# Block sums for two more gates and a branch, turns and residual loads on another queue, and half of w_out as a double block

## The chip, the cores and the metric

The kernel runs on one core of a Trainium2 chip. The metric is the device time of one execution in microseconds: the median of several timed runs. Beside them one execution was recorded by the profiler; all rows and durations below come from that one. TensorE multiplies matrices into PSUM, VectorE and ScalarE prepare operands and empty PSUM, GpSimd does a few additions, and SP only issues DMAs.

## What is computed

One layer of a hybrid decoder block, for 256 tokens of width 2048, in float32:

```python
h = rmsnorm(x, ln1_w)
proj = h @ w_in                       # q k v | pool input | z | xBC | dt | 3 gates of 2048
merged = (gates[0] * (att @ w_attn_br)      # branch 1, att is 1024 wide
        + gates[1] * (pool @ w_pool_br)     # branch 2, pool is 1024 wide
        + gates[2] * (ssm @ w_ssm_br))      # branch 3, ssm is 2048 wide
x = x + merged @ w_out                      # 2048 x 2048
h2 = rmsnorm(x, ln2_w)
gu = h2 @ w_gate_up                         # 2048 x 11264
x = x + (silu(gu[..., :5632]) * gu[..., 5632:]) @ w_down
return rmsnorm(x, final_w)
```

`gates` is the sigmoid of the last 6144 columns of `proj`.

## The kernel before

Every float32 operand is split into a rounded part `hi` and the rest `lo` (`split`, L139: a rounding on ScalarE, L142, and a difference on VectorE, L143), and a product is three matmuls, hi x hi, hi x lo and lo x hi (`three`, L220). Contraction runs over parts of 128 rows; 2048 rows are 16 of them. The 256 tokens are two tiles of 128, and columns go in blocks of 512. `tokens_block` (L226) makes one block of 512 columns for both token tiles: four rows of weights (1 MB) by one DMA into one of three buffers `raw`, split in two halves into `whi` and `wlo` (five buffers each), then 24 matmuls; a block of 16 rows has 96.

`two_blocks` (L312) makes two blocks of 512 columns at once, in eight pairs of rows. In six pairs it is the plain product, 24 matmuls. In the pairs 0 and 1 the four quarter products (two token tiles by two column blocks, over two rows) are made with seven products in place of eight, 21 matmuls, from sums of the weights (`block_weights`, L286, with the buffers `sraw`, `vu`, `shi`, `slo`) and sums of the activations (`block_forms`, L254). Its order of pairs is 0, 2, 3, 4, 1, 5, 6, 7, and after pair 1 VectorE combines the four accumulators that only the sums use. Before the change it serves `w_gate_up` and `w_down` alone.

PSUM has eight banks: `acc` (four), `tr` (two), `sm` (two). `k4` is a pool of 21 buffers of 4 KB per partition, which holds `h` (8), the parts of `ssm`, `mp` and `x2p` (8 each), `m4` (4), the gates, and others for a while. The pool `early` holds what the first stages use; it is closed after branch 3, and the pool `late` (`sraw`, `shi`, `slo`, `forms`) takes its place.

A block of tokens by channels that a later product contracts over has to be turned (`turn`, L490): 16 DMAs of 32 KB move it to `mid` (`move`), VectorE transposes 32x32 blocks, and it is split into the parts `hi` and `lo` (`parts`). These steps, and `forms_of`, don't stand where they are called: `later` (L120) queues them with a cost, `pause` queues a cost alone, and `side` (L126), called after each half of a weight load, adds a credit (1.4 for 1024 elements, capped at 4) and takes one step off the queue while the credit is positive. `need` (L205) takes steps until the part that is asked for is there. A program, which knows the dependencies, lays the instructions out on the engines and queues from this order.

The stages from 480 us on: branch 2 (gate and product for each of four blocks, L975), `z` and the scan's output with its turn into `ssm` (L985), branch 3 (L1001: two gates, then products and gates in turn; the sums `m4` are turned into `mp` from block 1 on, by SP), `w_out` with the residual (L1018: x loaded by SP into `x2`; four blocks, each turned into `x2p`), and the feed-forward part (L1055).

## Time and profile before

| | us |
|---|---|
| median of 3 timed runs | 1667.23 |
| lowest and highest of them | 1666.58, 1667.69 |
| the profiled execution | 1661.8 |
| its span, first to last instruction | 1660.0 |
| TensorE busy in it | 1632.7 (98%) |
| VectorE busy | 1247.3 (75%) |
| ScalarE busy | 879.0 (53%) |
| GpSimd busy | 59.3 (4%) |

Spans of matmuls overlap, since they are pipelined: the distance from one start to the next is what a matmul takes, not its shown duration. The last column of a row of the timeline, in brackets, is the idle time of the engine before it and what ended that. The window rows give for each engine the busy time in a stretch and the number of its instructions, then the granted share of TensorE's full clock, the busy share of the DMA engines and the GB/s.

### The profile page before, as it was taken

The numbers are of one execution on the slowest core, as the hardware profiler recorded it, in microseconds if no ns is written. First come the engines' busy times: TensorE is split into PE (matmuls) and PEld (weight loads), VectorE is DVE, ScalarE is ACT, GpSimd is POOL, SyncE is SP. The second block draws the span as 40 slices with busy tenths as digits, with TensorE's granted clock in tenths as the row PEclk, the third lists the DMA queues.
The fourth block names the chain that finished last, engine by engine and source line by source line (L and its number), as shares of the span: only waits on it lengthen the run. The fifth ranks groups of instructions, "written<-read, shape, count | busy, mean of one in ns | idle before, by whom it ended". The sixth has DMA issues, their size and how long they took to land.

```text
span 1660.0 us, 20771 instructions
## 1 busy us (share of the span) xinstructions
PE 1632.7 (98%) x7719; PEld 1355.8 (82%) x7719; DVE 1247.3 (75%) x1620; ACT 879.0 (53%) x1161; POOL 59.3 (4%) x58
## 2 busy tenths in 40 slices
PE   9999999999999999999969999999999999999997
PEld 8888888888888888888858888888888888888887
DVE  5789898955764457654547688988879888888986
ACT  6467678544444457544425555554445555445553
POOL 1000001200210000000000000000000000000000
PEclk9999999999999999999989999999999999999999
DMA  8654565556575656665567666666556666656663
GB/s 257 194 167 138 178 196 185 177 178 197 161 242 188 202 164 220 199 228 188 180 204 234 201 212 198 233 215 208 193 196 214 216 215 216 201 195 201 217 213 102
DMA packets 216901, 328.81 MB, mean 198 GB/s; under 512 B 15484, under 2 KB 89472, under 8 KB 216800
## 3 DMA queue, kind: packets, MB, share of 16 engines
q1 hardware_dynamic: 214496, 321.96, 59.5%
q0 software_dynamic: 1552, 4.66, 1.0%
q8 instruction: 60, 0.98, 0.2%
q10 hardware_dynamic: 752, 0.86, 0.2%
q14 instruction: 41, 0.34, 0.1%
HBM read 313.25 MB, written 2.13 MB: 190 GB/s over the span
## 4 chain that ended last, share of the span: by engine, by line
PE 82%; SPq 5%; DVE 5%; DMA 4%; ACT 2%; issue 2%; DVEq 0%; ACTq 0%
PE acc L222 11%; PE acc L223 11%; PE acc L224 11%; PE acc L376 9%; PE tr L222 6%; PE tr L224 5%; PE tr L223 5%; SPq L490 5%; PE sm L223 5%; PE sm L224 5%; PE sm L222 5%; PE acc L377 5%; DVE wlo L143 2%; DMA raw<-in_w_out_dram 1%; ACT whi L142 1%
## 5 line engine op out<-in xcount | busy, mean ns | idle before, releaser
L143 DVE TENSOR_TENSOR wlo<-raw,whi 128x1024 fp32r<-128x1024 f32 (+2 forms) x520 | 626.4, 1217 | 225.2 <-ACT whi L142 220.1
L142 ACT CAST whi<-raw 128x1024 fp32r<-128x1024 f32 (+2 forms) x520 | 529.7, 1035 | 393.5 <-PE acc L224 221.8
L376 PE MATMUL acc<-h,whi 128*128 128x512 f32 x640 | 228.8, 401 | 0.0
L222 PE MATMUL acc<-whi,h 128*128 128x512 f32 (+1 forms) x544 | 210.8, 389 | 2.1 <-DVE sg L920 0.8
L223 PE MATMUL acc<-wlo,h 128*128 128x512 f32 (+1 forms) x544 | 209.2, 385 | 0.6 <-DVE wlo L143 0.5
L224 PE MATMUL acc<-whi,h 128*128 128x512 f32 (+1 forms) x544 | 208.2, 385 | 0.1
L377 PE MATMUL acc<-h,wlo 128*128 128x256 f32 x640 | 180.7, 282 | 0.0
L376 PEld LDWEIGHTS acc<-h,whi 128*128 128x128 f32 x640 | 120.5, 188 | 30.1 <-issue 1.5
L377 PEld LDWEIGHTS acc<-h,wlo 128*128 128x128 f32 x640 | 121.0, 189 | 1.8 <-issue 1.8
L222 PEld LDWEIGHTS acc<-whi,h 128*128 128x128 f32 x544 | 102.0, 188 | 24.2 <-issue 2.3
L222 PE MATMUL tr<-whi,x2p_hi 128*128 128x512 f32 x308 | 120.8, 392 | 0.0
L224 PE MATMUL tr<-whi,x2p_lo 128*128 128x512 f32 x308 | 120.4, 391 | 0.0
L223 PEld LDWEIGHTS acc<-wlo,h 128*128 128x128 f32 x544 | 102.2, 188 | 22.3 <-DVE wlo L143 2.0
L223 PE MATMUL tr<-wlo,x2p_hi 128*128 128x512 f32 x308 | 120.3, 391 | 0.0
L224 PEld LDWEIGHTS acc<-whi,h 128*128 128x128 f32 x544 | 101.7, 188 | 20.7 <-DVE h L146 0.4
L142 ACT CAST whi<-sraw 128x1024 fp32r<-128x1024 f32 x64 | 67.1, 1049 | 90.7 <-PE sm L224 75.4
L143 DVE TENSOR_TENSOR wlo<-sraw,whi 128x1024 fp32r<-128x1024 f32 x64 | 78.2, 1221 | 33.4 <-ACT whi L142 33.2
L222 PE MATMUL sm<-whi,x2p_hi 128*128 128x512 f32 x264 | 102.8, 390 | 0.0
L223 PE MATMUL sm<-wlo,x2p_hi 128*128 128x512 f32 x264 | 102.8, 390 | 0.0
L224 PE MATMUL sm<-whi,x2p_lo 128*128 128x512 f32 x264 | 102.8, 390 | 0.0
L495 DVE STREAM_TRANSPOSE tt<-mid 128x512 f32<-128x512 f32 x46 | 47.3, 1066 | 54.7 <-DMA mid<-ff 18.1
L224 PEld LDWEIGHTS tr<-whi,x2p_lo 128*128 128x128 f32 x308 | 57.9, 188 | 12.8
(311 smaller groups left out, 2855.7 us busy)
## 6 DMA issues: line engine op xcount, KB each, us to landing
raw<-in_w_in_dram SPq DMA_DIRECT2D x104, 1024.0 KB, 5.3
raw<-in_w_gate_up_dram SPq DMA_DIRECT2D x132, 512.0 KB, 4.8
raw<-in_w_down_dram SPq DMA_DIRECT2D x62, 512.0 KB, 5.0
sraw<-in_w_gate_up_dram SPq DMA_DIRECT2D x44, 512.0 KB, 4.6
raw<-in_w_ssm_br_dram SPq DMA_DIRECT2D x16, 1024.0 KB, 5.8
raw<-in_w_out_dram SPq DMA_DIRECT2D x16, 1024.0 KB, 6.4
sraw<-in_w_down_dram SPq DMA_DIRECT2D x20, 512.0 KB, 5.0
raw<-in_w_attn_br_dram SPq DMA_DIRECT2D x8, 1024.0 KB, 5.0
```

The source lines that it names most:

```text
L142: a = act.copy(hi, src)
L143: b = dve.tensor_tensor(lo, src, hi.bitcast(F32), ALU.subtract)
L222: pe.matmul(o, lhsT=xh, rhs=yh, start=first, stop=False)
L223: pe.matmul(o, lhsT=xh, rhs=yl, start=False, stop=False)
L224: pe.matmul(o, lhsT=xl, rhs=yh, start=False, stop=last)
L376: pe.matmul(accs[c], lhsT=hi[:, j, cols], rhs=a.both(k), start=k == 0, stop=False)
L377: pe.matmul(accs[c][:, :SEQ], lhsT=lo[:, j, cols], rhs=a.hi(k), start=False, stop=k == KD - 1)
L490: sp.dma_start(mid[32 * j:32 * j + 32, i], block[32 * i:32 * i + 32, :, j * P:(j + 1) * P])
L495: dve.transpose(tt.rearrange("p k (t i s) -> p t i k s", t=T, i=4)[:, t], mid[:, :, t].rearrange("p i (c k) -> p i k c", k=4),)
```

## The change

- Two gates of branch 2 (blocks 1 and 2), all four gates of branch 3 and all four of its products are made by `two_blocks` with block sums: five double blocks (`two_gates` three times, `two_branches` twice) in place of ten plain blocks.
- `two_blocks` keeps the sums' accumulators in `tr` and `sm` and the others in `acc` (before: the other way round), and takes no forms when `forms` is None: all eight pairs are then plain. The first two blocks of `w_out` are one such double block.
- The four turns of `m4` and the four loads of x into `x2` are issued on GpSimd's queue in place of SP's. Blocks 0 and 1 of `m4` are turned after the last gates, 2 and 3 after the last product. The turns of `x2` stay on SP; those of blocks 0 and 1 now follow each other after the double block.
- `early` is closed and `late` opened before branch 2's products. `vu` moves to `late` with one buffer in place of two, and `k4` has 22 buffers.

```diff
--- before.py
+++ after.py
@@ -87,7 +87,7 @@
 
 
     def k4(shape, dt=F32, name="k4"):
-        return work.tile([P, *shape], dt, tag="k4", name=name, bufs=21)
+        return work.tile([P, *shape], dt, tag="k4", name=name, bufs=22)
 
     def k2(shape, dt=F32, name="k2", tag="k2", bufs=6):
         return work.tile([P, *shape], dt, tag=tag, name=name, bufs=bufs)
@@ -183,6 +183,9 @@
         def __init__(self, n, name):
             self.t = [k4([2, 2, SEQ], F32R, name) for _ in range(n // 2)]
 
+        def need(self, k):
+            pass
+
         def both(self, k):
             return self.t[k // 2][:, k % 2].rearrange("p a s -> p (a s)")
 
@@ -223,17 +226,14 @@
         pe.matmul(o, lhsT=xh, rhs=yl, start=False, stop=False)
         pe.matmul(o, lhsT=xl, rhs=yh, start=False, stop=last)
 
-    def tokens_block(a, nk, loads_of, cols, loaded=None):
-
-        accs = [acc() for _ in range(T)]
+    def tokens_block(a, nk, loads_of, cols, accs=None):
+
+        accs = accs or [acc() for _ in range(T)]
         step = 8 if cols <= 256 else 4
         for i in range(0, nk, step):
             n = min(step, nk - i)
-            if isinstance(a, Parts):
-                a.need(i)
+            a.need(i)
             pieces = weights(loads_of(i, n), [n, cols])
-            if loaded is not None:
-                loaded(i)
             for s, e, hi, lo in pieces:
                 for t in range(T):
                     tok = slice(t * P, (t + 1) * P)
@@ -275,20 +275,23 @@
             later(lambda p=p: forms_of(p), 3.0)
         return out
 
-    def block_loads(w, k, c1, c2):
+    def block_loads(w, k, cols, moved):
 
         k0 = k // 4 * 4
         return [
-            ((lambda r, j=j: r[:, 2 * j:2 * j + 2, :]), turned(w, k0, 4, c, NB)[0][1][:, k - k0:k - k0 + 2, :])
-            for j, c in enumerate((c1, c2))
+            (
+                (lambda r, j=j: r[:, 2 * j:2 * j + 2, :]),
+                turned(w, k0, 4, c, NB)[0][1][:, k - k0:k - k0 + 2, :] if moved else rows(w, k, 2, c, NB),
+            )
+            for j, c in enumerate(cols)
         ]
 
-    def block_weights(w, k, c1, c2):
+    def block_weights(loads):
 
         raw = late.tile([P, 4, NB], F32, tag="sraw", name="sraw", bufs=1)
-        for to, src in block_loads(w, k, c1, c2):
+        for to, src in loads:
             sp.dma_start(to(raw), src)
-        vu = wpool.tile([P, 2, NB], F32, tag="vu", name="vu", bufs=2)
+        vu = late.tile([P, 2, NB], F32, tag="vu", name="vu", bufs=1)
         out = []
 
         def part(src):
@@ -309,16 +312,20 @@
         out.append((hi, lo))
         return out
 
-    def two_blocks(a, forms, w, k0, c1, c2, nk):
-
-
-
-        q1, q7, q5, q6 = acc(), acc(), acc(), acc()
-        q2, q4, q3, q8 = tr(), tr(), sm(), sm()
-        seven = [0, 1]
-        plain = list(range(2, nk // 2))
-        share = len(plain) // len(seven)
-        order = []
+    def two_blocks(a, forms, w, k0, cols, nk, moved=True):
+
+
+
+        if forms is None:
+            q2, q4, q3, q8 = tr(), tr(), sm(), sm()
+            seven, s1, u2, u3, s5 = [], None, None, None, None
+        else:
+            q1, q7, q5, q6 = tr(), tr(), sm(), sm()
+            q2, q4, q3, q8 = acc(), acc(), acc(), acc()
+            seven = [0, 1]
+        plain = list(range(len(seven), nk // 2))
+        share = len(plain) // max(len(seven), 1)
+        order = [] if seven else plain
         for i, p in enumerate(seven):
             order += [p] + plain[i * share:(i + 1) * share]
         for p in order:
@@ -328,7 +335,7 @@
                 while p not in forms:
                     tasks.popleft()[0]()
                 f = forms[p]
-                b11, b21, v, u, z, w_, b22 = block_weights(w, k0 + ka, c1, c2)
+                b11, b21, v, u, z, w_, b22 = block_weights(block_loads(w, k0 + ka, cols, moved))
                 first, last = p == seven[0], p == seven[-1]
                 tok = [slice(t * P, (t + 1) * P) for t in range(T)]
 
@@ -356,14 +363,14 @@
                     dve.tensor_tensor(s5, q5, u2, ALU.subtract)
                     dve.tensor_tensor(u2, q5, u3, ALU.subtract)
             else:
-                for j, (_, _, hi, lo) in enumerate(weights(block_loads(w, k0 + ka, c1, c2), [4, NB])):
+                for j, (_, _, hi, lo) in enumerate(weights(block_loads(w, k0 + ka, cols, moved), [4, NB])):
                     for t in range(T):
                         q = ((q2, q4), (q3, q8))[j][t]
                         for k in range(2):
                             xh, xl = a.hi(ka + k)[:, t * P:(t + 1) * P], a.lo(ka + k)[:, t * P:(t + 1) * P]
                             three(
                                 q, xh, xl, hi[:, k], lo[:, k],
-                                q is q8 and p == plain[0] and k == 0, p == plain[-1] and k == 1,
+                                (q is q8 or not seven) and p == plain[0] and k == 0, p == plain[-1] and k == 1,
                             )
                     side(0.9 * 1024 * SHARE)
         return ((q2, s1), (q4, u3)), ((q3, s5), (q8, u2))
@@ -477,7 +484,7 @@
                     last = split(p[:, k, :], dst.hi(kt), dst.lo(kt), scale(kt))
         return last
 
-    def turn(block, k0, dst, scale=None, wait=5.0):
+    def turn(block, k0, dst, scale=None, queue=sp):
 
 
 
@@ -487,7 +494,7 @@
         def move():
             for i in range(4):
                 for j in range(4):
-                    sp.dma_start(mid[32 * j:32 * j + 32, i], block[32 * i:32 * i + 32, :, j * P:(j + 1) * P])
+                    queue.dma_start(mid[32 * j:32 * j + 32, i], block[32 * i:32 * i + 32, :, j * P:(j + 1) * P])
 
         def parts():
             tt = k4([4, SEQ], F32, "tt")
@@ -505,7 +512,7 @@
             dst.waiting.discard(k0 // 4)
 
         later(move)
-        pause(wait)
+        pause(5.0 if queue is sp else 12.0)
         later(parts, 3.8)
 
 
@@ -909,16 +916,36 @@
             act.activation(sg[:, t, :], a, AF.Sigmoid, scale=rstd1[:, t:t + 1])
         return sg
 
-    def branch(br, j, a_parts, w, sg, loads=plain_loads):
+    def two_gates(br, j):
+
+        c0 = C_G + br * D + j * NB
+        out = []
+        for sums in two_blocks(h, h_forms, w_in, 0, (c0, c0 + NB), KD, False):
+            sg = k4([T, NB], F32, "sg")
+            for t, (q, more) in enumerate(sums):
+                dve.tensor_tensor(more, q, more, ALU.add)
+                act.activation(sg[:, t, :], more, AF.Sigmoid, scale=rstd1[:, t:t + 1])
+            out.append(sg)
+        return out
+
+    def branch(br, j, a_parts, w, sg, banks=None):
         if br == 0:
             m4.append(k4([T, NB], F32, "m"))
         nk = w.shape[0] // P
-        for t, a in enumerate(tokens_block(a_parts, nk, loads(w, 0, j * NB, NB), NB)):
+        for t, a in enumerate(tokens_block(a_parts, nk, plain_loads(w, 0, j * NB, NB), NB, banks)):
             if br == 0:
                 dve.tensor_tensor(m4[j][:, t, :], a, sg[:, t, :], ALU.mult)
             else:
                 dve.tensor_tensor(sg[:, t, :], a, sg[:, t, :], ALU.mult)
-                (dve if br == 2 else pool).tensor_tensor(m4[j][:, t, :], m4[j][:, t, :], sg[:, t, :], ALU.add)
+                pool.tensor_tensor(m4[j][:, t, :], m4[j][:, t, :], sg[:, t, :], ALU.add)
+
+    def two_branches(j, sgs):
+
+        for n, sums in enumerate(two_blocks(ssm, s_forms, ins["w_ssm_br"][0], 0, (j * NB, (j + 1) * NB), KD)):
+            for t, (q, more) in enumerate(sums):
+                dve.tensor_tensor(more, q, more, ALU.add)
+                dve.tensor_tensor(more, more, sgs[n][:, t, :], ALU.mult)
+                dve.tensor_tensor(m4[j + n][:, t, :], m4[j + n][:, t, :], more, ALU.add)
 
     for j in range(4):
         sg = gate(0, j)
@@ -972,12 +999,16 @@
             later(lambda pair=pair: pool_mix(pair), 2.4)
             pair = []
 
-    sg_pool = [gate(1, 0)]
+    sg = gate(1, 0)
     finish_tasks()
-    for j in range(4):
-        if j:
-            sg_pool.append(gate(1, j))
-        branch(1, j, po, ins["w_pool_br"][0], sg_pool[j])
+    early_pool.close()
+    late = ctx.enter_context(tc.tile_pool(name="late", bufs=1))
+    h_forms = block_forms(h, (0, 1))
+    branch(1, 0, po, ins["w_pool_br"][0], sg)
+    sgs = two_gates(1, 1)
+    branch(1, 1, po, ins["w_pool_br"][0], sgs[0], [tr(), tr()])
+    branch(1, 2, po, ins["w_pool_br"][0], sgs[1], [sm(), sm()])
+    branch(1, 3, po, ins["w_pool_br"][0], gate(1, 3))
 
 
     ssg = tiny([T, GROUPS], "ssg", 1)
@@ -998,38 +1029,44 @@
         later(finish, 1.5)
         turn(ys[g], 4 * g, ssm, lambda k: norms[:, 0, k:k + 1])
 
-    sg_ssm = [gate(2, j) for j in range(2)]
+        if g == 0:
+            s_forms = block_forms(ssm, (0, 1))
+
+    sgs = two_gates(2, 0)
     finish_tasks()
-    for j in range(4):
-        branch(2, j, ssm, ins["w_ssm_br"][0], sg_ssm[j], turned_loads)
-        if j + 2 < 4:
-            sg_ssm.append(gate(2, j + 2))
-        if j == 1:
-            mp = Parts(KD, "mp")
-            for i in range(2):
-                turn(m4[i], 4 * i, mp)
-        elif j > 1:
-            turn(m4[j], 4 * j, mp)
-
-    early_pool.close()
-    late = ctx.enter_context(tc.tile_pool(name="late", bufs=1))
+    two_branches(0, sgs)
+    sgs = two_gates(2, 2)
+    mp = Parts(KD, "mp")
+    for j in range(2):
+        turn(m4[j], 4 * j, mp, queue=pool)
+    two_branches(2, sgs)
+    for j in range(2, 4):
+        turn(m4[j], 4 * j, mp, queue=pool)
 
 
     x2 = []
     for j in range(4):
         xj = k4([T, NB], F32, "x2")
-        sp.dma_start(xj, x_in[:, :, j * NB:(j + 1) * NB])
+        pool.dma_start(xj, x_in[:, :, j * NB:(j + 1) * NB])
         x2.append(xj)
     ss2 = tiny([T, 4], "ss2", 1)
     x2p = Parts(KD, "x2p")
-    for j in range(4):
-        for t, a in enumerate(tokens_block(mp, KD, turned_loads(ins["w_out"][0], 0, j * NB, NB), NB)):
+    forms = []
+
+    def residual(j, accs):
+        for t, a in enumerate(accs):
             dve.tensor_tensor(x2[j][:, t, :], a, x2[j][:, t, :], ALU.add)
             junk = k2([NB], F32, "junk")
             act.activation(junk, x2[j][:, t, :], AF.Square, accum_out=ss2[:, t, j:j + 1])
         turn(x2[j], 4 * j, x2p, lambda k: norms[:, 1, k:k + 1])
         if j == 0:
-            forms = block_forms(x2p, (0, 1))
+            forms.append(block_forms(x2p, (0, 1)))
+
+    w_out = ins["w_out"][0]
+    for n, sums in enumerate(two_blocks(mp, None, w_out, 0, (0, NB), KD)):
+        residual(n, [q for q, _ in sums])
+    for j in range(2, 4):
+        residual(j, tokens_block(mp, KD, turned_loads(w_out, 0, j * NB, NB), NB))
     ssum2 = tiny([T], "ssum2", 1)
     dve.tensor_reduce(ssum2, ss2, AX.X, ALU.add)
     rstd2 = rsqrt(ssum2, D, [T], "rs2")
@@ -1056,7 +1093,7 @@
         f = Parts(4 * len(some), "f")
         for i, b in enumerate(some):
             a_ = k4([T, NB], F32, "ff")
-            gates, ups = two_blocks(x2p, forms, wgu, 0, b * NB, DFF + b * NB, KD)
+            gates, ups = two_blocks(x2p, forms[0], wgu, 0, (b * NB, DFF + b * NB), KD)
             for t, (q, more) in enumerate(gates):
                 dve.tensor_tensor(more, q, more, ALU.add)
                 act.activation(a_[:, t, :], more, AF.Silu, scale=rstd2[:, t:t + 1])
@@ -1083,14 +1120,14 @@
                 )
                 fw.extend(fw4[:, c, :] for c in range(4))
         for j in (0,) if last else (0, 2):
-            sums = two_blocks(f, f_forms, wd, k0, j * NB, (j + 1) * NB, nk)
+            sums = two_blocks(f, f_forms, wd, k0, (j * NB, (j + 1) * NB), nk)
             for n in range(2):
                 for q, more in sums[n]:
                     dve.tensor_tensor(more, q, more, ALU.add)
             for n in range(2):
                 down(j + n, 0, NB, j + n if last else None, [more for _, more in sums[n]])
-    down(2, 0, NB, 2, tokens_block(f, nk, turned_loads(wd, k0, 2 * NB, NB), NB))
-    down(3, 0, 256, 3, tokens_block(f, nk, turned_loads(wd, k0, 3 * NB, 256), 256))
+    down(2, 0, NB, 2, tokens_block(f, nk, turned_loads(wd, k0, 2 * NB, NB), NB, [tr(), tr()]))
+    down(3, 0, 256, 3, tokens_block(f, nk, turned_loads(wd, k0, 3 * NB, 256), 256, [sm(), sm()]))
 
 
     wl = []
```

## Rows read from the trace of the kernel before

**Rows 1.** The page's head: busy time by engine, and TensorE's clock by slice.

```profile
PE 1632.7 (98%) x7719; PEld 1355.8 (82%) x7719; DVE 1247.3 (75%) x1620; ACT 879.0 (53%) x1161; POOL 59.3 (4%) x58
...
PEclk9999999999999999999989999999999999999999
```

**Rows 2.** Waits of TensorE, 450 to 1640 us: total, times, longest.

```profile
PE acc L222 <- ACT whi L142: 11.6, 2, 11.0
PE acc L223 <- DVE wlo L143: 1.6, 3, 0.8
PE acc L222 <- DVE sg L920: 0.8, 2, 0.4
PE acc L222 <- DVE x L1027: 0.5, 1, 0.5
```

**Rows 3.** Windows: branch 3's stage, the start of w_out, one feed-forward block.

```profile
700.00:840.00 140.00, 138.76 (x609) 113.65 (x608) 76.38 (x70) 61.76 (x63) 0.00 (x0) 1.00 0.62 196
840.00:880.00 40.00, 27.55 (x112) 21.40 (x111) 21.90 (x21) 13.52 (x14) 0.00 (x0) 0.87 0.76 255
1076.00:1119.00 43.00, 43.00 (x190) 35.36 (x189) 36.81 (x41) 22.47 (x25) 0.00 (x0) 1.00 0.63 213
```

**Rows 4.** Timeline of TensorE: start, duration, line, tiles; w_out's borders and two half blocks.

```profile
845.16 0.39 PE L224 MATMUL acc<-whi,ssm_lo 128*128 128x512 f32 x1
...
939.26 0.39 PE L222 MATMUL acc<-whi,mp_hi 128*128 128x512 f32 x1
...
939.94 0.39 PE L222 MATMUL acc<-whi,mp_hi 128*128 128x512 f32 x1
...
947.42 0.39 PE L222 MATMUL acc<-whi,x2p_hi 128*128 128x512 f32 x1
...
1076.33 0.39 PE L222 MATMUL acc<-whi,x2p_hi 128*128 128x512 f32 x1
...
1097.57 0.39 PE L222 MATMUL acc<-whi,x2p_hi 128*128 128x512 f32 x1
```

**Rows 5.** Timeline of SP's queue, 820 to 905 us.

```profile
825.89 13.21 SPq L490 DMA_DIRECT2D mid<-m  x16
839.20 1.29 SPq L153 DMA_DIRECT2D raw<-in_w_out_dram  x2
...
852.17 10.30 SPq L490 DMA_DIRECT2D mid<-m  x16
862.56 19.93 SPq L153 DMA_DIRECT2D raw<-in_w_out_dram  x7
```

**Rows 6.** Timeline of VectorE: the last sum of m4[3], and its transposes.

```profile
851.42 0.69 DVE L921 TENSOR_TENSOR m<-m,sg 128x512 f32<-128x512 f32 x1
...
863.98 2.04 DVE L495 STREAM_TRANSPOSE tt<-mid 128x512 f32<-128x512 f32 x2 [10.74 <-DMA mid<-m]
```

**Rows 7.** Timeline of VectorE: beside GpSimd at 212 us, and a weight sum.

```profile
212.68 2.06 DVE L143 TENSOR_TENSOR wlo<-raw,whi 128x1024 fp32r<-128x1024 f32 x1
...
1066.60 1.22 DVE L301 TENSOR_TENSOR vu<-sraw 128x1024 f32<-128x1024 f32 x1
```

**Rows 8.** Timeline of GpSimd: DMA issues and additions.

```profile
6.41 0.77 POOL L550 DMA_DIRECT2D norms<-in_ssm_norm_w_dram  x1 [0.69 <-DMA heads<-in_dt_bias_dram]
...
72.77 0.56 POOL L664 DMA_DIRECT2D upto_rows<-rows  x1 [64.55 <-ACT rows L663]
...
213.61 1.12 POOL L804 DMA_DIRECT2D mt<-upto_rows  x2
...
255.63 1.28 POOL L878 TENSOR_TENSOR y<-y,off 128x512 f32<-128x512 f32 x1 [40.90 <-DVE off L876]
...
323.27 2.14 POOL L878 TENSOR_TENSOR y<-y,off 128x512 f32<-128x512 f32 x1 [10.37 <-DVE off L876]
```

**Rows 9.** DMA issues: tiles, queue, times, size of each, us to landing (median).

```profile
mid<-m SPq DMA_DIRECT2D x64, 32.0 KB, 1.9
...
upto_rows<-rows POOLq DMA_DIRECT2D x1, 32.0 KB, 2.0
```

## The prediction

> **What bounds the kernel now.** First the page's head and its clock row: TensorE is busy 98% of the span and its clock is full in every slice but one [rows 1]. So time can come only from fewer matmuls or from TensorE's few idle stretches. Next the waits of TensorE from 450 us to 1640 us: 14.5 us in eight waits, 11.0 of them in one [rows 2]. Then the windows: of the 40 us from 840 us TensorE was busy 27.55, with the clock at 0.87; before it hardly anything is lost, and from 1076 us nothing [rows 3]. That one place is the start of `w_out`. Branch 3's last matmul starts at 845.16, the first of the feed-forward part at 947.42 [rows 4]. Matmuls of plain blocks start 0.227 us apart (three take 0.68, [rows 4]); between the two lie the 384 of `w_out`, 87.05 us. From 845.39 (845.16 + 0.227) to 947.42 are 102.03 us: the stage loses **15.0 us**.
>
> Its cause stands in SP's queue. It issues the 16 moves of `m4[2]` from 825.89 and so reaches `w_out`'s first loads only at 839.20; the moves of `m4[3]` hold it until 862.56, and only then comes the load of the third four rows of `w_out` [rows 5]. `m4[3]` itself was complete on VectorE only at 852.1 [rows 6]: SP stood in order behind it. TensorE runs out of weights for the 11.0 us of [rows 2]; the clock of 0.87 in this window [rows 3] is a second price of the pause, and both are in the 15.0.
>
> **The change part by part.** All times are of the profiled execution, 1661.8 us with a span of 1660.0; the median of the timed runs, 1667.23, is 5.4 us above it, and I carry the difference over unchanged.
>
> *Five double blocks with block sums* (three of gates, two of branch 3), where ten plain blocks stood. Each takes 42 matmuls in place of 48 for two of its eight pairs. I take the price from the feed-forward part, which runs the same code: its half blocks (93 matmuls) begin 21.24 us apart [rows 4], so a double block is 42.48 us against 192 x 0.2267 = 43.52. That is 1.04 us, not the 1.36 that six matmuls would give, because the matmuls of the pairs with sums start further apart. 5 x 1.04 = **5.2 us**. The bounds are 3 (a join that costs 0.4 us each time) and 6.8 (30 x 0.227).
>
> Their extra work lies on VectorE. A pair with sums needs three differences of 1024 elements, one sum of 1024, and three operations of 512: 4 x 1.22 + 3 x 0.69 = 6.95 us [rows 6, 7], a plain pair 2.44. Per double block: 6 x 2.44 + 2 x 6.95 + four combinations and four final sums of 0.69 = 34 us of 42.5. In the gates' stage VectorE was busy 55%; in the feed-forward part, which carries these blocks and a turn and the SwiGLU products, 36.81 of 43 us, and TensorE still never waited [rows 3]. So I cost it at nothing; the cover is the two to three pairs by which weight pieces run ahead (five buffers of halves). The four forms of `h` and of `ssm` are made in plain stages before them. The ends are covered too: the next block's first 12 matmuls (2.7 us) go to other banks than those being emptied. Two waits of gates for a branch's banks (0.8 us together) and the one of 0.5 us at the feed-forward part's start [rows 2] go, because the double blocks begin in banks that were emptied half a block earlier: **1.3 us**. The other short waits I leave.
>
> *Turns of m4 and loads of x on GpSimd's queue.* 64 moves and four loads leave SP, which then only loads weights in this stage; SP no longer stands behind `m4[3]`, and the 16 x 0.64 us that a turn took of it are gone [rows 5]. What GpSimd asks instead: the one row of the same shape (32 partitions, 32 KB, rows of 512 B) was issued in 0.56 us [rows 8] and landed after 2.0 us, against 1.9 for a move on SP [rows 9]. The dearest issue shown is 0.77 us [rows 8]. I take 0.56, since the shape is the same. The row at 6.41 also shows the ninth DMA waiting 0.69 us for the first to land [rows 8]: as if eight could be in flight. Eight moves take 4.5 us to issue and each lands in 2, so this does not bind; it would if the loads of x, sixteen times as large, stood right before them, but these wait only for buffers, and `h` gives back eight after the last gates, a whole double block earlier.
>
> *w_out's first half as a double block.* It saves no matmul. It uses each part of `mp` for twice the work: with t as the end of branch 3's last matmul, part 2 is needed at pair 4, t + 4 x 5.44 = t + 21.8, and part 3 at pair 6, t + 32.6. The supply: blocks 2's and 3's sums need twelve VectorE operations of 0.69; the banks of `m4[2]` are final 2.7 us before t, so I put it at t + 2 and `m4[3]` at t + 6. Moves of `m4[2]`: 16 x 0.56 = 9.0, to t + 11, landed t + 13. Then the transposes, 2.04 [rows 6], ScalarE's rounding and VectorE's difference of 1024 elements, 1.22 each at most [rows 7], 4.4 us in all: t + 17.4, **4.4 us early**. `m4[3]`: issued to t + 20, landed t + 22, ready t + 26.4, **6.2 us early**. Parts 0 and 1 come from blocks finished a double block earlier. What is queued behind a late part: the differences of the next weight pieces, which stand behind the transposes on VectorE. With none late, the 15.0 us go.
>
> *What is late next.* `x2[0]` and `x2[1]` now come together, 43.5 us into `w_out`, and their turns stay on SP, 16 issues of 0.64 us each [rows 5]. By the planner's costs (8 x 1.4 a plain block; a turn costs 8.8, the forms 6) the first part and both forms are placed by the end of `w_out`'s third and fourth block, part 1 at the second pair of the feed-forward part, and the moves of `x2[2]` and `x2[3]` inside its first block; they are needed at its fourth pair (15.6 us) and seventh (31 us). SP has the time: 41 us of issue in some 75 us, beside loads of 1.3 us for each 5.4. VectorE is the tighter one: up to three turns of some 3.7 us (2.04 of transposes and four differences that are at least the 1.22 of one) come on the 34 us of that block, 45 of 42.5 if all fall into it. Before, this start lost 0.5 us for VectorE [rows 2]. I add 1 us, with bounds of 0 and 5, and 0.5 us for the joins of the gates' stage (0 to 2).
>
> Sum: -5.2 - 1.3 - 15.0 + 1.0 + 0.5 = **-20.0 us**: 1641.8 us in the profiled execution, **1647** against the median.
>
> **A rule that speaks against it.** GpSimd's tensor operations do stretch beside VectorE: the same addition took 1.28 us once and 2.14 another time, and a difference of VectorE took 2.06 in place of 1.22 beside one; but the two DMA issues that came right after it took 0.56 each beside differences of VectorE [rows 7, 8]. The Trainium skill, SBUF — State Buffer, sections "SBUF: two separate sides" and "Who interferes with whom", says that a DMA issued on GpSimd starves while VectorE runs a copy or `tensor_scalar` in a mode that takes both ports, 0.62 us becoming 3.1, and advises SP or ScalarE for a DMA to be hidden under VectorE; it excepts `tensor_tensor`. By 3.1 us sixteen moves would take 50 us and the change would lose. No row here shows an issue of that length, and VectorE runs `tensor_tensor` and transposes at this place.
>
> **The rivals.** With an issue of c us on GpSimd, part 3 is ready at t + 2 + 32c + 2 + 4.4 and stalls TensorE from c = 0.76 on, by 32c - 24.2.
> 1. *GpSimd's issues stretch as its additions do*, by 2.14 / 1.28 = 1.7 to 0.93 us: a stall of 5.6 us, **1653**. For it: VectorE is busiest there. Against: the two issues of 0.56.
> 2. *The turns of x2 pile up* at the start of the feed-forward part: SP or VectorE late by the ends above, 5 us, and the joins at 2: **1652 to 1656**. For it: 41 us of moves in the second half of the stage instead of spread over it. Against: SP idles otherwise, and weights run five loads ahead.
> 3. *Slower: each issue on GpSimd first waits for a VectorE instruction to end*, 1.22 + 0.56 = 1.78 us at the start of `w_out`: a stall of 32.8 us in place of the 15.0, so **1679**. It decides from c = 1.39 on, where the stall of 20.3 eats everything won. The skill's rule above would come out there.
> 4. *The stall is not the queue's*: the order of SP and VectorE is laid out by a planner, and `w_out` could again start late for want of a part of `mp`. Then only the 6.5 us of matmuls and banks are left: **1661**. Against: in rows 5 the load follows the moves without a pause.
>
> **How the numbers follow.** A measurement of this kernel can tell about 0.2% (3.3 us) from no change. Forecast 0.70 (1644 to 1650), rival 1 0.09, rival 2 0.11, rival 4 0.05, rival 3 0.04, and 0.01 for a tie in between. The lower end is all terms at their best (6.8 + 1.75 + 15.0 = 23.5, so 1643.7); the upper one takes in rivals 1 and 2, 1656. Faster: 0.70 + 0.09 + 0.11 + 0.04 of rival 4 = 0.94; same 0.02; slower 0.04.
>
> **What would show it.** Right: 30 matmuls fewer; no wait of TensorE over 2 us near 830 to 870 us, with the clock full there; the double blocks of gates 42.5 us long; GpSimd's moves 0.53 to 0.6 us apart, landing in about 2. Wrong: moves over 0.76 us apart and a wait at the fifth or seventh pair of `w_out`; waits for VectorE in the first feed-forward block; differences of 2 us beside GpSimd's issues.

## The result, and the profile after

| | before | changed |
|---|---|---|
| median of 4 timed runs | 1666.90 us | 1646.68 us |
| lowest and highest | 1663.82, 1667.69 | 1645.22, 1648.74 |
| the profiled execution | 1661.8 us | 1648.74 us |

The ratio is 0.9883, with a 95% interval of 0.9866 to 0.9900: 20.2 us faster, where 20.0 were forecast. The two profiled executions, however, are only 13.1 us apart. The number was right, in part by luck: the sum behind it was not right term by term, and most of what follows is about that.

The page's head of the changed kernel, for [rows 1]; 30 matmuls fewer, and a full clock in every slice:

```profile
PE 1626.4 (99%) x7689; PEld 1349.5 (82%) x7689; DVE 1318.8 (80%) x1738; ACT 898.2 (55%) x1190; POOL 96.8 (6%) x126
...
PEclk9999999999999999999999999999999999999999
```

TensorE's waits from 450 to 1640 us, for [rows 2] (total, times, longest), and its timeline at the borders of the stages, for [rows 4]:

```profile
PE acc L226 <- DVE wlo L143: 6.9, 4, 3.9
```

```profile
668.65 0.39 PE L225 MATMUL tr<-whi,h 128*128 128x512 f32 x1
...
681.24 0.50 PE L226 MATMUL acc<-wlo,h 128*128 128x512 f32 x1 [1.84 <-DVE wlo L143]
...
706.68 0.50 PE L226 MATMUL acc<-wlo,h 128*128 128x512 f32 x1 [3.87 <-DVE wlo L143]
...
719.09 0.39 PE L225 MATMUL tr<-whi,ssm_hi 128*128 128x512 f32 x1
...
761.58 0.39 PE L225 MATMUL tr<-whi,h 128*128 128x512 f32 x1
...
846.57 0.39 PE L225 MATMUL tr<-whi,mp_hi 128*128 128x512 f32 x1
...
933.61 0.39 PE L225 MATMUL tr<-whi,x2p_hi 128*128 128x512 f32 x1
```

Two things can be seen here. `w_out` takes 87.04 us (846.57 to 933.61), what its 384 matmuls need: nothing is left of its 15.0 us. And two new waits stand at 681 and 706 us, inside the first double block of branch 3's gates: it lasts from 668.65 to 719.09, 50.44 us, while the next one takes 42.49. After the second wait the clock is low for a while; the windows (for [rows 3]; the columns are those of that group):

```profile
706.00:712.00 6.00, 5.32 (x16) 4.25 (x17) 6.00 (x6) 1.23 (x2) 0.00 (x0) 0.72 0.58 190
...
840.00:880.00 40.00, 40.00 (x178) 33.15 (x177) 32.31 (x35) 16.91 (x17) 17.07 (x32) 1.00 0.65 202
```

From first matmul to first matmul of each stage, in us, for two recorded executions of each kernel (the second ones are the runs `b2` and `a2` below) and for the best version found (`splityx`); before the change, branch 3 ends where its last matmul's successor could have started:

| | branch 2's products | z | branch 3 | w_out | to the end |
|---|---|---|---|---|---|
| before | 108.80 | 87.05 | 176.54 | 102.03 | 712.6 |
| before, again | 108.80 | 87.05 | 176.83 | 104.26 | 711.9 |
| changed | 107.77 | 87.04 | 177.92 | 87.04 | 713.0 |
| changed, again | 107.77 | 87.04 | 176.73 | 87.04 | 712.1 |
| turns shared | 107.78 | 87.04 | 170.68 | 87.04 | 710.8 |

Branch 3's stage has four of the five double blocks and gained nothing by them.

**Where the new waits come from.** VectorE and SP in the changed kernel around them, for [rows 5, 6]:

```profile
672.25 2.06 DVE L502 STREAM_TRANSPOSE tt<-mid 128x512 f32<-128x512 f32 x2 [3.76 <-DMA mid<-y]
...
699.49 1.09 DVE L502 STREAM_TRANSPOSE tt<-mid 128x512 f32<-128x512 f32 x1 [4.88 <-DMA mid<-y]
...
705.40 4.62 DVE L143 TENSOR_TENSOR wlo<-raw,whi 128x1024 fp32r<-128x1024 f32 x4
```

```profile
659.82 10.77 SPq L497 DMA_DIRECT2D mid<-y  x16
...
686.42 11.50 SPq L497 DMA_DIRECT2D mid<-y  x16
```

The transposes of `ssm`'s last two turns stand on VectorE in front of weight differences, and VectorE idles 3.8 and 4.9 us for moves that SP needs 11 us to issue. Behind the second one come the transposes and the combinations of the block sums; the next weight difference is at 705.40, and TensorE has run dry. VectorE had work that was ready: the next two weight pieces were rounded by 695.4 and 696.8, and their differences are the first two of the four that start at 705.40.

```profile
694.38 1.05 ACT L142 CAST whi<-raw 128x1024 fp32r<-128x1024 f32 x1 [0.55 <-ACT s L360]
695.73 1.05 ACT L142 CAST whi<-raw 128x1024 fp32r<-128x1024 f32 x1 [0.29 <-PE acc L227]
```

At the first wait SP's queue has a share of its own. The piece that TensorE waits for there was loaded only right behind the moves and rounded at 677.14:

```profile
670.68 1.04 SPq L153 DMA_DIRECT2D raw<-in_w_in_dram  x2
```

```profile
677.14 1.03 ACT L142 CAST whi<-raw 128x1024 fp32r<-128x1024 f32 x1
```

VectorE idled at these turns before the change too, and TensorE hardly noticed: the two gates there lost 1.1 us (44.65 us for 192 matmuls, which need 43.52). From the kernel before:

```profile
672.31 2.06 DVE L495 STREAM_TRANSPOSE tt<-mid 128x512 f32<-128x512 f32 x2 [3.67 <-DMA mid<-y]
...
695.51 2.06 DVE L495 STREAM_TRANSPOSE tt<-mid 128x512 f32<-128x512 f32 x2 [5.12 <-DMA mid<-y]
```

That a double block with its sums has no such reserve is the theory which the experiments test.

### The profile page after: what moved, and what is told of

Its sections match the earlier page's. It is cut to its first block, busy times and chain, and to the rows that moved or that the text cites. A ratio compares the mean times of both kernels' runs of the same rounds, so it can differ in the third digit from the quotient of the medians.

```text
span 1646.6 us, 20971 instructions
## 1 busy us (share of the span) xinstructions
PE 1626.4 (99%) x7689; PEld 1349.5 (82%) x7689; DVE 1318.8 (80%) x1738; ACT 898.2 (55%) x1190; POOL 96.8 (6%) x126
## 4 chain that ended last, share of the span: by engine, by line
PE 86%; SPq 4%; DMA 4%; DVE 3%; issue 1%; ACT 1%; DVEq 0%; ACTq 0%
PE acc L225 19%; PE acc L227 19%; PE acc L226 19%; PE acc L383 9%; PE acc L384 4%; SPq L497 4%; PE sm L226 2%; PE tr L227 2%; PE tr L226 2%; PE tr L225 2%; PE sm L225 2%; PE sm L227 2%; DVE wlo L143 1%; DMA raw<-in_w_gate_up_dram 1%; PE sm L868 1%
## 5 line engine op out<-in xcount | busy, mean ns | idle before, releaser
L143 DVE TENSOR_TENSOR wlo<-raw,whi 128x1024 fp32r<-128x1024 f32 (+2 forms) x500 | 600.2, 1215 | 155.8 <-ACT whi L142 154.7
L226 PE MATMUL acc<-wlo,x2p_hi 128*128 128x512 f32 x572 | 223.2, 390 | 1.2 <-DVE wlo L143 1.2
L225 PE MATMUL acc<-whi,x2p_hi 128*128 128x512 f32 x572 | 223.3, 390 | 0.0
L227 PE MATMUL acc<-whi,x2p_lo 128*128 128x512 f32 x572 | 223.0, 390 | 0.0
L225 PE MATMUL acc<-whi,h 128*128 128x512 f32 (+1 forms) x508 | 196.9, 390 | 2.3 <-ACT whi L142 1.9
L227 PE MATMUL acc<-whi,h 128*128 128x512 f32 (+1 forms) x508 | 194.6, 386 | 0.0
L226 PEld LDWEIGHTS acc<-wlo,x2p_hi 128*128 128x128 f32 x572 | 107.4, 188 | 25.0 <-DVE wlo L143 2.3
L227 PEld LDWEIGHTS acc<-whi,x2p_lo 128*128 128x128 f32 x572 | 107.4, 188 | 23.0
L225 PEld LDWEIGHTS acc<-whi,x2p_hi 128*128 128x128 f32 x572 | 107.3, 188 | 23.0
L226 PEld LDWEIGHTS acc<-wlo,h 128*128 128x128 f32 x508 | 95.8, 189 | 26.4 <-DVE wlo L143 7.2
L225 PE MATMUL acc<-whi,f_hi 128*128 128x512 f32 x244 | 95.3, 391 | 0.0
L227 PE MATMUL acc<-whi,f_lo 128*128 128x512 f32 x244 | 95.1, 390 | 0.0
```

Of the source, the lines that this page charges most:

```text
L143: b = dve.tensor_tensor(lo, src, hi.bitcast(F32), ALU.subtract)
L225: pe.matmul(o, lhsT=xh, rhs=yh, start=first, stop=False)
L226: pe.matmul(o, lhsT=xh, rhs=yl, start=False, stop=False)
L227: pe.matmul(o, lhsT=xl, rhs=yh, start=False, stop=last)
```

## The experiments

The theory (A): three causes add up. SP's queue and the late need of `mp` both count at `w_out`; the sums are worth what the feed-forward part shows; and the new loss comes from `ssm`'s turns. The rivals: at `w_out` only one of the two counts; the new loss is VectorE's work of the sums itself. Ratios are to the kernel before on the same chip; times of runs on different chips are compared by them.

**The two kernels again.**

> The kernel before once more, for a second profile: the recorded execution of before (1661.8 us) was shorter than every timed one (1663.8 to 1667.7). If w_out's delay of 15.0 us is steady, it is 14 to 16 us here too and the difference to the median lies in the stages before it; if it is w_out's delay that varies, it is 17 to 20 us.

1663.48 us, one execution. TensorE's waits (total, times, longest; a comment line on top shifts this kernel's line numbers by one):

```profile
PE acc L223 <- ACT whi L143: 10.4, 2, 8.2
```

Its `w_out` took 104.26 us, 17.2 over its matmuls (15.0 in the first record), split otherwise: the long wait is 8.2 us in place of 11.0, the one at the start 2.2 in place of 0.7, and the clock from 840 to 880 us 0.79 in place of 0.87. So the delay is not steady. The recorded execution was again shorter than the median (1666.91); whether the rest of that difference sits at `w_out` too is not shown.

> The changed kernel once more: 1646 to 1648 us. Its profile lost 7.9 us in the first double block of branch 3's gates (50.44 us in place of 42.49) and nothing at w_out. If these are steady, the block takes 48 to 52 us here too; if they come and go, under 45.

1646.47 us, 0.9880 (0.9865 to 0.9895). The block lost 6.8 us (49.25 in place of 42.49), `w_out` nothing. The loss is steady, and its size moves by a microsecond: in `spq`, `wplain` and `copies` below, which leave this block as it is, it takes 49.1 to 50.4 us.

**SP's queue against the double block at w_out.**

```diff
-        turn(m4[j], 4 * j, mp, queue=pool)
+        turn(m4[j], 4 * j, mp)
...
-        turn(m4[j], 4 * j, mp, queue=pool)
+        turn(m4[j], 4 * j, mp)
...
-        pool.dma_start(xj, x_in[:, :, j * NB:(j + 1) * NB])
+        sp.dma_start(xj, x_in[:, :, j * NB:(j + 1) * NB])
```

> The changed kernel with the turns of m4 and the loads of x back on SP's queue (and with the pause of 5 that goes with SP). If SP's standing in order behind m4 made the delay, it comes back in part: 5 to 11 us of waiting at w_out, 1652 to 1658 us. If the double block of w_out alone is the cure, because every part of mp is needed twice as late, it loses 2 us at most: 1646 to 1649 us.

1652.10 us, 0.9911 (0.9895 to 0.9928): 5.6 us of the gain lost. SP's timeline, and TensorE's:

```profile
846.07 10.62 SPq L497 DMA_DIRECT2D mid<-m  x16
856.73 1.61 SPq L153 DMA_DIRECT2D raw<-in_w_out_dram  x3
858.38 12.12 SPq L497 DMA_DIRECT2D mid<-m  x16
870.60 19.07 SPq L153 DMA_DIRECT2D raw<-in_w_out_dram  x10
```

```profile
876.33 0.81 PE L225 MATMUL tr<-whi,mp_hi 128*128 128x512 f32 x2 [3.69 <-ACT whi L142]
```

The picture of [rows 5] is back: the load behind the moves comes at 870.60, and TensorE waits for it; `w_out` takes 93.10 us.

```diff
-    for n, sums in enumerate(two_blocks(mp, None, w_out, 0, (0, NB), KD)):
-        residual(n, [q for q, _ in sums])
-    for j in range(2, 4):
+    for j in range(4):
         residual(j, tokens_block(mp, KD, turned_loads(w_out, 0, j * NB, NB), NB))
```

> The changed kernel with all four blocks of w_out plain, and the turns of m4 on GpSimd. Parts 2 and 3 of mp are then needed 10.9 and 16.3 us after branch 3 ends; by the changed kernel's profile they are ready after 19.5 and 31.2. So the theory that the supply counts expects some 15 us of waiting and 2 us of lower clock: 1661 to 1664 us. If only SP's queue made the delay, it is 1647 to 1650 us.

1657.87 us, 0.9947 (0.9932 to 0.9962): 11.4 us lost, not the 15 to 17 expected. `w_out` takes 97.84 us. The long wait is for a part of `mp` now; the short one before it is for weights whose load landed late beside the moves, as ScalarE's row shows:

```profile
857.79 0.73 PE L225 MATMUL acc<-whi,mp_hi 128*128 128x512 f32 x2 [1.91 <-ACT whi L142]
...
863.24 0.80 PE L225 MATMUL acc<-whi,mp_hi 128*128 128x512 f32 x1 [4.71 <-ACT mp_hi L142]
```

```profile
856.70 1.04 ACT L142 CAST whi<-raw 128x1024 fp32r<-128x1024 f32 x1 [2.44 <-DMA raw<-in_w_out_dram]
```

From the kernel before, the queue alone (with its pause of 12):

```diff
...
-                turn(m4[i], 4 * i, mp)
+                turn(m4[i], 4 * i, mp, queue=pool)
...
-            turn(m4[j], 4 * j, mp)
+            turn(m4[j], 4 * j, mp, queue=pool)
...
-        sp.dma_start(xj, x_in[:, :, j * NB:(j + 1) * NB])
+        pool.dma_start(xj, x_in[:, :, j * NB:(j + 1) * NB])
```

> The kernel before with one part of the change: turns of m4 and loads of x on GpSimd's queue (with its pause of 12). If SP's queue alone makes the delay at w_out, 15 to 17 us go: 1650 to 1653 us. If the supply of mp counts as much, as the run with plain blocks of w_out (10.8 us left) says, 5 to 7 us go: 1660 to 1662 us.

1654.51 us, 0.9942 (0.9922 to 0.9961): 9.7 us by the ratio, 11.9 by the medians, between both expectations. `w_out` takes 94.05 us, with one long wait, for the last part:

```profile
866.28 0.79 PE L222 MATMUL acc<-whi,mp_hi 128*128 128x512 f32 x1 [5.36 <-ACT mp_hi L142]
```

So neither alone cures it. With SP's queue the stage loses 6.1 us, with plain blocks 10.8, with neither 15.0 and 17.2, with both 0.0. In the changed kernel the plain blocks cost more than in the kernel before (10.8 against 7.0), because the double block of branch 3 finishes blocks 2 and 3 of `m4` together: their moves start at 846.16 and right behind that in `wplain`, at 828.35 and 849.95 in `bpool`. The double block of `w_out` also pays for that.

**The new loss.** The double blocks kept, all pairs plain:

```diff
-        for sums in two_blocks(h, h_forms, w_in, 0, (c0, c0 + NB), KD, False):
+        for sums in two_blocks(h, None, w_in, 0, (c0, c0 + NB), KD, False, [acc() for _ in range(4)]):
...
-        for n, sums in enumerate(two_blocks(ssm, s_forms, ins["w_ssm_br"][0], 0, (j * NB, (j + 1) * NB), KD)):
+        for n, sums in enumerate(two_blocks(ssm, None, ins["w_ssm_br"][0], 0, (j * NB, (j + 1) * NB), KD)):
...
```

(Not shown: the additions of the sums' parts and the two `block_forms` go too.)

> The changed kernel with the five double blocks kept, but all eight pairs plain: no block sums, 30 matmuls more, no sums of weights or forms on VectorE. In the changed kernel the first double block of branch 3's gates loses 6 to 8 us. If the sums' work on VectorE makes that loss, it goes: +5.2 - 6 = 1645 to 1647 us. If it comes from the last turn of ssm, whose transposes stand in front of weight differences and wait for the moves, 3 us or more of it stay: 1649 to 1652 us.

1650.48 us, 0.9908 (0.9894 to 0.9923). The time is as theory A has it, but the run doesn't part the two cleanly: the gates' block loses 6.2 us in one wait at another place:

```profile
678.26 0.79 PE L225 MATMUL acc<-whi,h 128*128 128x512 f32 x1 [4.60 <-ACT sz L1016]
```

Without sums this block takes the `acc` banks at once, and one of them is emptied only when ScalarE has done `ssm`'s part 2, which waits for the same moves. So the late moves cost about as much without any sums. The wait at 706 us is gone, though VectorE idles 5.1 us there: that one needs the turn and the sums' work together.

Later transposes, by one number:

```diff
-        pause(5.0 if queue is sp else 12.0)
+        pause(wait if queue is sp else 12.0)
...
-        turn(ys[g], 4 * g, ssm, lambda k: norms[:, 0, k:k + 1])
+        turn(ys[g], 4 * g, ssm, lambda k: norms[:, 0, k:k + 1], wait=8.0 if g == 3 else 5.0)
```

> The changed kernel with one number changed: the pause between the moves and the transposes of the last turn of ssm is 8 in place of 5, so that the planner places the transposes two weight pairs later. If the waiting transposes make the wait of 2 to 4 us at 706 us, it goes, and with it the clock's dip: the block loses 2 to 3 us, 1642 to 1644 us. If VectorE's work of the sums makes it, nothing changes: 1646 to 1647 us.

1645.86 us, 0.9882 (0.9867 to 0.9896): no difference that can be told. The wait at 706 us went, as expected, though only the second of the two transposes moved (from 701.07 to 705.43) and VectorE still idled 3.3 us in front of the first. The two expected microseconds did not come: the block still lost 4.7 us, and the next one 2.2 to small waits, of which this was one:

```profile
722.33 0.50 PE L226 MATMUL acc<-wlo,ssm_hi 128*128 128x512 f32 x1 [0.76 <-DVE wlo L143]
```

Earlier turns, by the order of the steps:

```diff
-        if g == 0:
+        if g == 3:
             s_forms = block_forms(ssm, (0, 1))
```

> The changed kernel with the forms of ssm queued behind its last turn and not behind the first. 6 credits of steps leave the stage of z, so the turns of ssm parts 1 and 2 come some 10 us earlier there. If the late turns make the loss, both waits at 681 and 706 us shrink: the block loses under 3 us, 1642 to 1644 us. If not, 1646 to 1648 us.

1647.77 us, 0.9892 (0.9878 to 0.9907): a miss. The moves of parts 1, 2 and 3 went out 3.7, 1.3 and 1.5 us earlier (the last at 684.94 in place of 686.42), not 10: in both kernels each set starts when VectorE has finished its block of `ys`. And the forms now fell into the crowded block. Placing the same work elsewhere moves the loss; it does not remove it.

Faster moves, half of each turn's 16 on either queue:

```diff
-                    queue.dma_start(mid[32 * j:32 * j + 32, i], block[32 * i:32 * i + 32, :, j * P:(j + 1) * P])
+                    (pool if queue is None and j % 2 else queue or sp).dma_start(mid[32 * j:32 * j + 32, i], block[32 * i:32 * i + 32, :, j * P:(j + 1) * P])
...
-        turn(ys[g], 4 * g, ssm, lambda k: norms[:, 0, k:k + 1])
+        turn(ys[g], 4 * g, ssm, lambda k: norms[:, 0, k:k + 1], None)
```

> The changed kernel with the 16 moves of each turn of ssm issued half on SP and half on GpSimd, which is idle there. In the changed kernel each set takes SP 10 to 11.5 us, and VectorE idles 3.8 and 4.9 us in front of the transposes at 672 and 699 us. If the waits at 681 and 706 us come from these transposes standing in front of weight differences, moves that are there some 4 us earlier take most of them: the block's loss falls from 6 to 8 us to under 3, 1641 to 1644 us. If VectorE's extra work of the sums is the cause by itself, it stays at 1646 to 1647 us.

1642.19 us, 0.9865 (0.9850 to 0.9880). Against the 0.9880 of `a2` this is 2.5 us, and the intervals overlap; the profile is clearer. The block takes 43.11 us, 6 to 7 us less than in both records of the changed kernel, and both waits are gone, with all the sums' work in place. (The next block lost 0.6 us of it, and the feed-forward start 0.7 to 1.6 more than before.) So the late moves are the cause. That the sums' work only took the reserve fits all runs, but is argued. Shared moves also leave SP free for its loads some 6 us earlier (5.1 us of issue in place of 10.8 and 11.5): how much of the wait at 681 us that was, and how much VectorE's waiting, this run does not part.

With the turns of x2 as well:

```diff
-        turn(x2[j], 4 * j, x2p, lambda k: norms[:, 1, k:k + 1])
+        turn(x2[j], 4 * j, x2p, lambda k: norms[:, 1, k:k + 1], None)
```

> As the run before it, with the turns of x2 shared in the same way. The first two feed-forward blocks lost 1.3 to 2.1 us in the changed kernel. If the moves on SP make that, 1 us or so is won on top of the run before; if VectorE is simply full there, nothing.

1638.66 us, 0.9844 (0.9827 to 0.9860): the best version. Against 0.9880 and 0.9883 for the changed kernel it is 6.0 to 6.5 us faster, clear of the intervals; the medians, from different chips, are 8 us apart. The first two feed-forward blocks, which lost 2.8 us in `splity`, lose nothing here: VectorE is not simply full there, and faster moves are enough. They are not the only way: in `nosums`, with all these moves on SP, the two blocks lost nothing either, and why is open. TensorE's only wait from 450 to 1640 us, and the transposes that had idled 4.9 us:

```profile
PE acc L226 <- DVE wlo L143: 0.2, 1, 0.2
```

```profile
691.10 2.08 DVE L502 STREAM_TRANSPOSE tt<-mid 128x512 f32<-128x512 f32 x2 [2.39 <-DMA mid<-y]
```

**The price of the sums,** in that version, where no late move hides it: the edit of `nosums` on top of `splityx`.

> The kernel with the turns of ssm and x2 shared between SP and GpSimd (1638.7 us, 0.9844 of before), with the five double blocks all plain: no block sums there. The prediction priced the sums at 1.04 us a double block, by the feed-forward part's half blocks: 5.2 us, so 1643 to 1645 us and 0.987 to 0.988 of before. If the sums cost their gain again in the joins, it stays at 1638 to 1640 us.

1644.18 us, 0.9877 (0.9857 to 0.9896): 5.5 us slower than with the sums (5.2 by the sum). The intervals just overlap, but the profiles agree: 5.6 us between the spans, and 43.52 us in place of 42.49 for a double block without waits. The first double block of branch 3's gates loses 1.2 us here, against 6.2 in `nosums`: with or without sums, the loss follows the moves.

**GpSimd's issues beside copies on VectorE.**

```diff
     two_branches(2, sgs)
+    for _ in range(12):
+        dve.tensor_copy(k2([NB], F32, "copy"), m4[3][:, 0, :])
```

> The changed kernel with twelve float32 copies of 512 elements, SBUF to SBUF, added on VectorE right behind the sums of m4[3]: work that nobody needs, beside GpSimd's moves. By the changed kernel's rows (64 issues, 0.54 us each, beside additions and differences) the issues stay at 0.54 to 0.6. If a copy on VectorE keeps GpSimd from issuing, those beside copies take 1 us or more.

Its timelines of GpSimd and VectorE, and the window of the copies:

```profile
849.64 4.45 POOL L497 DMA_DIRECT2D mid<-m  x1
```

```profile
849.88 4.11 DVE L1044 COPY copy<-m 128x512 f32<-128x512 f32 x12
```

```profile
849.88:854.00 4.12, 4.12 (x20) 3.41 (x19) 4.12 (x14) 1.05 (x2) 4.12 (x1) 1.00 0.03 8
```

One issue that fell on the copies took 4.45 us, until all twelve were done; the 16 moves took 12.46 us in place of 8.51, and TensorE then waited 1.6 us for a part of `mp`. The expectation of 0.54 to 0.6 held beside additions and differences only. (The run is one execution, 1650.53 us.)

## Why the prediction was right, and where its sum was not

- **The w_out delay: right in mechanism.** It went to nothing, and `spq` and `bpool` show SP's queue as one of its two causes. The forecast named the supply of `mp` as the condition; `wplain` shows it to be the other cause. Its 15.0 us were one execution's; another had 17.2.
- **The bank waits: right.** The rows for 0.8 and 0.5 us in [rows 2] have no counterpart in the changed kernel, whose waits are all for weight differences.
- **The timeline of the turns: too early.** `m4[2]` was ready at t + 19.5 (forecast t + 17.4, needed t + 21.8), `m4[3]` at t + 31.2 (t + 26.4, t + 32.6): 1.4 us of slack where 6.2 were claimed. The step that failed is the landing, as the rows show:

```profile
792.71 4.25 POOL L497 DMA_DIRECT2D mid<-m  x8 [0.99 <-DMA mid<-m]
...
847.89 8.51 POOL L497 DMA_DIRECT2D mid<-m  x16 [41.94 <-ACT whi L142]
857.15 0.54 POOL L497 DMA_DIRECT2D mid<-m  x1 [0.74 <-issue]
858.63 1.60 POOL L497 DMA_DIRECT2D mid<-m  x3 [0.95 <-DMA mid<-m]
```

```profile
mid<-y SPq DMA_DIRECT2D x64, 32.0 KB, 1.9
...
mid<-m POOLq DMA_DIRECT2D x64, 32.0 KB, 4.7
```

  The issue took 0.53 us (forecast 0.56); the median landing was 4.7 us and not 2.0. Then eight in flight do bind (8 x 0.53 is 4.3): the first row is the second half of a turn, held until a move had landed, and the turn of `m4[3]` took 11.3 us to issue, 0.70 a move. So rivals 1 and 3 fell, with no issue over 0.60 us, and what rival 4 feared, a late part of `mp`, came within 1.4 us.
- **The block sums: right.** 5.2 us by half blocks, 5.5 measured. The 6.8 us of a count of matmuls would have been too much.
- **The joins: the mis-sized term.** 0.5 us, bounded by 2; measured 6.8 and 8.0 us, all in the first double block of branch 3's gates. Some of that was there before: the stage was to win 4.5 us (four blocks 4.2, banks 0.8, joins -0.5), and it lost 1.4 in the first records and won 0.1 in the second, so the sum was 4.4 to 5.8 us off here. The step that failed is the one that cost the sums' work at nothing. I covered the sums' work by the feed-forward part, where TensorE never waits at 86% of VectorE, and did not look at what waits on VectorE in the stage it came to: [rows 6] shows VectorE idle in front of a transpose at `w_out`, and the same stood at the turns of `ssm`, 3.7 and 5.1 us. Rival 2 had the mechanism, VectorE and SP late for a turn, but put it at x2's.
- **The feed-forward start:** 1.0 us forecast. Together the first two blocks took 1.4 us (first record) and 0.8 us (second) more than their matmuls before, 2.1 and 1.3 after: 0.6 us.
- **The execution and the median: a second error that hid the first, by luck.** I carried the 5.4 us between record and median over. The changed kernel's record lay 2.1 us above its median instead. The sum was 7 us too good for the recorded pair (20.0 against 13.1; 0.8 of that lies ahead of branch 2), and the offset 7 us too bad. With the second records the pair is 17.4 us apart.
- **Where the offset probably lies: at `w_out`.** Up to `w_out` the two records of the kernel before agree within 0.2 us, and there they differ by 2.2. Of its 30 timed executions beside the runs, those with a granted clock of 0.995 took 1663.1 us in the mean, those with 0.994 1666.3 and with 0.993 1667.4; and in both records, but for the last 20 us, the clock is under 1.00 from 840 to 950 us alone (0.95 and 0.92). So the delay that went was probably longer in the median than the 15.0 of the sum. The timed executions have no trace, so this is not shown.
- **Two slips that changed nothing.** Rival 3's own terms give 1680 us, not 1679, and the 1.75 us in the lower end of the range is worked out nowhere.

## What to carry to other kernels

When work is added to an engine, look in that stage for instructions on it that wait for a DMA with other work queued behind them: busy shares don't show that the reserve is needed there. A turn of many small DMAs is as late as its issue is long, and sharing the issue between two queues cured what shifting the work around did not. Take a delay that varies from more than one record before it goes into a sum. Cut a delay's causes apart by undoing each one alone: here each alone left 6 to 11 us.

## What the runs showed of the hardware

- **Small transfers land later among others.** The windows of SP's moves before the change, and of GpSimd's after it:

```profile
852.20:862.40 10.20, 6.23 (x28) 4.84 (x26) 1.04 (x1) 0.00 (x0) 0.00 (x0) 1.00 0.23 54
```

```profile
857.00:868.00 11.00, 11.00 (x50) 9.13 (x49) 6.57 (x7) 4.96 (x5) 8.15 (x16) 1.00 0.83 245
```

  While SP issues moves it issues no loads: the DMA engines moved 54 GB/s, and a move landed in 1.9 us. Beside SP's loads, at 245 GB/s, one from GpSimd took 4.7. In `splityx` the moves of `ssm` landed in 1.8 to 2.2 us and those of x2 in 3.6 to 3.7, on either queue alike. One turn of the changed kernel shows that it is the other traffic and not the queue. SP issued its next load at 852.05; the first six moves of the turn, from 847.89 on, landed in 1.7 to 2.5 us, and its last eight, issued behind that load, in 4.3 to 5.9 (lowest, median, highest; then the windows):

```profile
DMA to landing us min/median/max: 1.7/1.8/2.5
```

```profile
DMA to landing us min/median/max: 4.3/5.6/5.9
```

```profile
847.90:850.50 2.60, 2.60 (x13) 2.14 (x12) 2.60 (x5) 1.02 (x1) 2.60 (x5) 1.00 0.16 38
852.00:863.00 11.00, 11.00 (x50) 9.12 (x49) 6.01 (x7) 3.17 (x3) 8.78 (x18) 1.00 0.93 288
```

- **A copy on VectorE stops GpSimd's DMA issue.** Twelve copies back to back held one issue for 4.45 us, while 64 issues beside additions, differences and transposes took 0.54 (0.60 at most). The Trainium skill, SBUF — State Buffer, sections "SBUF: two separate sides" and "Who interferes with whom", says both: copies starve it, `tensor_tensor` does not. The runs agree, so the change rests on VectorE having no such work beside the moves.
- **A pause of TensorE can cost more than its length.** After the wait of 3.87 us eight matmuls started 0.43 us apart (the lower of the clock's two levels, 1.2 GHz), some 1.6 us on top; the granted clock of that window is the 0.72 shown above. In `a2` the same came after the first wait, of 1.99 us (0.72 from 681 to 687 us), and not after the second, of 2.04.
